# Seven block products for eight in every third pair of W_up's row tiles

## The chip, the cores and the metric

One core of a Trainium2 chip runs the whole program. The metric is the device time of one execution in microseconds (us), as the median of several runs.

## The reference

Two encoder layers on x of 512 positions by 1024 features. Each layer first mixes a Fourier group and windowed attention into x, and then runs the convolutional FFN, which is where the change lies (D_FF = 2816):

```python
h = rmsnorm(x, norm2[l])
up = dwconv_centred(h @ w_up[l], conv_w[l], conv_b[l])   # three taps along the positions
gate, val = up[..., :D_FF], up[..., D_FF:]
x = x + (jax.nn.silu(gate) * val) @ w_down[l]
```

W_up has 2 x 2816 columns, thus 44 row tiles of 128 in the transposed layout of the kernel. Tile fi of the gate and tile fi + 22 of the value belong together: a pair.

## The kernel before

Everything is kept transposed: features on the 128 partitions, the 512 positions along the free dimension. x is 8 tiles of 128 x 512. Inputs are float32, and the matmuls take operands of the reduced type fp32r. So each operand is split into a high part (a rounded copy, by ACT, line 101 or 137) and a low part (what is left, by DVE, line 102 or 140), and one product is three matmuls: high x high, low x high, high x low (`mm3`, lines 114 to 122). Weights are the stationary operand, and each matmul loads its own.

A tile of W_up (1024 x 128) is loaded as one transfer of 512 KB into `wraw` (3 buffers), split in two chunks of 512 columns into `whi` and `wlo` (5 buffers each, lines 132 to 141), and used for 8 contraction steps of 3 matmuls, 128 x 512 each, into one PSUM bank. The row scale 1/rms of h is applied afterwards (`rb2`, line 719), since it is a factor of each position. Then ACT does the middle tap and bias, DVE the two outer taps (lines 721 to 723). For a pair, ACT takes silu of the gate's tile, the two are multiplied (line 728: on DVE in layer 0, on POOL in layer 1), and the result is split into a high and a low part and kept as W_down's right operand.

The 22 pairs are done in two halves of 11 (`HALVES`, line 35). After each half comes W_down's part of it: for each of the 8 output tiles, 11 contraction steps of 3 matmuls into one bank, and an add into x (line 756). The kept operands lie in `slab`, `pT` and `m4` (lines 729 to 737). The last output tile of the last half is done in two halves of 256 positions (lines 748 to 756).

While layer 0's FFN runs, `presplit` (lines 149 to 198) prepares layer 1's weights other than W_up and W_down: it loads them, folds some of them on DVE, splits them (ACT and DVE, through `tA`) and stores both parts in DRAM. One step of it is taken at every `next(ahead)`: two in three pairs of tiles, and two for each output tile of W_down.

The order on each engine is fixed ahead of time by the framework's scheduler (line 841): it goes by the order of the program, and takes a later instruction where an earlier one is not ready by its own estimate. Each engine then runs its list in order. The accumulators of the FFN rotate over 6 PSUM banks (`FFN_BANKS`, line 34).

Of the kernel before, what the change touches and what calls it, by code (L numbers as in the profile page):

```python
# [31 lines left out]
NWARM = 10  # L32
RATE, STEP0 = 1, 12
FFN_BANKS = ("mm", "mm", "mm", "av", "sc", "sc")
HALVES = [(0, 11), (11, 11)]


def encoder_kernel(tc, t):
# [29 lines left out]
    def f(x):  # L68
# [2 lines left out]

    BANKS = {"mm": 3, "sc": 2, "tp": 2, "av": 1}
    TEMPS = {"act": (1024, 8), "m4": (1024, 5), "slab": (1024, 4), "pT": (2560, 2),
             "tA": (512, 6), "tF": (512, 6), "sq": (512, 2)}
# [14 lines left out]
    def act(out, in_, func=AF.Copy, **kw):  # L89
        return nc.scalar.activation(out, in_, func, **kw)  # L90
# [36 lines left out]
    def wload(src, n, raw=None):  # L127
        raw = wtile() if raw is None else raw
        nc.sync.dma_start(raw[:, :n], src)
        return raw[:, :n]  # L130

    def wsplit(raw, eng=None, hi_eng=None):
        hi = wp.tile([P, 512], F32R, tag="whi", name=nm("whi"), bufs=5)
        lo = wp.tile([P, 512], F32R, tag="wlo", name=nm("wlo"), bufs=5)
        n = raw.shape[-1]
        if hi_eng is None:
            act(hi[:, :n], raw)
        else:
            hi_eng.tensor_copy(hi[:, :n], raw)
        tt(lo[:, :n], raw, f(hi)[:, :n], ALU.subtract, eng)  # L140
        return hi, lo

    def wchunks(src, n, step=512, eng=None):
        raw = wload(src, n)
        return [wsplit(raw[:, c:min(c + step, n)], eng) for c in range(0, n, step)]
# [3 lines left out]
    def presplit(l):  # L149

        late = []

        def keep(key, src):
            n = src.shape[-1]
            two = [temp(n, "tA", F32R) for _ in range(2)]
            split(two[0], two[1], src)
            kept[key] = [dp.tile([P, n], F32, tag=f"{key}{s}", name=nm("kept")) for s in range(2)]
            store()
            late.append(lambda: [nc.sync.dma_start(o, f(z)) for o, z in zip(kept[key], two)])

        def store():
            while late:
                late.pop()()

        def cols(src, n, step):
            def load():
                raw = temp(1024, "m4")
                nc.sync.dma_start(raw[:, :n], src)
                return [raw[:, c:c + step] for c in range(0, n, step)]
            return load  # L170

        def prepare(kind, raw):
            if kind == "u":
                return fold_wu(raw)
            return fold_wf(raw) if kind == "f" else raw

        jobs = []
        for grp in (1, 0):
            for kk in range(KT // 2):
                jobs.append((cols(t["w_qkv"][l, grp, kk], 768, 384), [f"qkv{grp}{2 * kk + i}" for i in range(2)]))  # L180
        for kk in range(KT // 2):
            jobs.append((lambda kk=kk: load_wu(l, kk, temp(1024, "m4")), [f"u{2 * kk + i}" for i in range(2)]))
        for j in range(NF):
            jobs.append((lambda j=j: [load_wf(l, j, temp(1024, "m4"))], [f"f{j}"]))
        for half in range(2):
            for mp in range(KT // 2):
                jobs.append((cols(t["w_o"][l, half, :, mp * 1024:(mp + 1) * 1024], 1024, 512),
                             [f"o{half}{2 * mp + i}" for i in range(2)]))
        got = jobs[0][0]()
        for n, (_, keys) in enumerate(jobs):  # L190
            for i, key in enumerate(keys):
                keep(key, prepare(key[0], got[i]))
                if i == len(keys) - 1 and n + 1 < len(jobs):
                    got = jobs[n + 1][0]()
                yield
        store()
        while True:
            yield
# [66 lines left out]
    mask = cut(pb, 3 * P)  # L265


    zero = temp(512, "sq")
    nc.vector.memset(zero, 0.0)
    warm = temp(512, "sq", F32R)  # L270
    act(warm, zero)
    wps = psum("sc")
    for _ in range(NWARM):
# [44 lines left out]
        return tab, alt, wt  # L318


    def add_square(acc, src, first, tag="sq"):
# [46 lines left out]
    def load_wu(l, kk, raw=None):  # L368

        raw = wtile() if raw is None else raw  # L370
        nc.sync.dma_start(raw.rearrange("p (k c) -> p k c", k=2),
                          t["w_in"][l, 2 * kk * P:2 * (kk + 1) * P, 0:FW].rearrange("(k p) c -> p k c", p=P))
        return [raw[:, k * 512:(k + 1) * 512] for k in range(2)]

    acc = accum()
    xg = [norm_tile(k, g1[:, 0, :], acc) for k in range(KT)]

    for l in range(L):
# [323 lines left out]
        if l == 0:  # L702
            tabs, alts, wt = load_tables(1)
        ahead = presplit(l + 1) if l < L - 1 else iter(lambda: 0, 1)
        for f0, nf in HALVES:
            gu = []
            for fi in range(f0, f0 + nf):
                ys_ = []
                n = fi - f0
                for z in range(2):  # L710
                    m = fi + z * FT
                    w = wchunks(t["w_up"][l, m], 1024)
                    nps[0] += 1
                    o = psum(FFN_BANKS[nps[0] % len(FFN_BANKS)])
                    for k in range(KT):
                        mm3(o, [q[:, (k % 4) * P:(k % 4 + 1) * P] for q in w[k // 4]], [h2[k][:, s, :] for s in range(2)],
                            k == 0, k == KT - 1)
                    u = temp(512, "tF")
                    tt(u, o, rb2, ALU.mult)
                    y = temp(512, "tF")  # L720
                    act(y, u, AF.Identity, scale=cw[:, l, 1, m:m + 1], bias=cb[:, l, m:m + 1])
                    stt(y[:, 1:], u[:, :-1], cw[:, l, 0, m:m + 1], y[:, 1:], ALU.mult, ALU.add)
                    stt(y[:, :-1], u[:, 1:], cw[:, l, 2, m:m + 1], y[:, :-1], ALU.mult, ALU.add)
                    ys_.append(y)
                    if (2 * n + z) % 3 == 2:
                        next(ahead)
                act(ys_[0], ys_[0], AF.Silu)
                tt(ys_[0], ys_[0], ys_[1], ALU.mult, nc.gpsimd if l else nc.vector)
                if n < 4:
                    a = pair("slab")  # L730
                elif n < 8:
# [3 lines left out]
                else:  # L735
                    a = pair("m4")
                split(a[:, 0, :], a[:, 1, :], ys_[0])
                gu.append(a)
            nxt = []
            for m in range(KT):  # L740
                next(ahead)
                next(ahead)
                w = []
                for c in range(0, nf, 8):
                    n = min(8, nf - c)
                    w += wchunks(t["w_down"][l, m, :, (f0 + c) * P:(f0 + c + n) * P], n * P)
                end = l == L - 1 and f0 + nf == FT
                nh = 2 if end and m == KT - 1 else 1
                for h in range(nh):
                    q0, q1 = h * S // nh, (h + 1) * S // nh  # L750
                    nps[0] += 1
                    o = psum(FFN_BANKS[nps[0] % len(FFN_BANKS)])[:, q0:q1]
# [97 lines left out]
```

## Time and profile before

| | |
|---|---|
| median of 3 runs | 1057.46 us (1056.27 to 1057.54) |
| profiled execution | 1056.14 us, its span 1054.3 us |
| FFN of layer 0 | from about 190 to 535 us of the span |
| FFN of layer 1 | from about 705 us to the end |
| DMA share in the span | 40.5% of 16 engines (queue q1) |

The profile is one execution. PE is TensorE, DVE is VectorE, ACT is ScalarE, POOL is GpSimd, SP is the engine that issues the transfers. The page gives the busy time of each engine, the chain of work that ended last, and the costliest groups of instructions: line, engine, operation, output<-input, count, then busy us, mean ns of one, and idle time ahead of it with what ended it. A table by stretches has the length first, then busy us (x instructions) for PE, PEld (weight loads), DVE, ACT and POOL, then the granted clock, the DMA share and GB/s. A timeline row has start, duration, engine, line, operation; the idle time before it and its releaser stand in brackets. A row "x2" merges two instructions. Matmuls overlap: the distance between starts is their price, not the duration.

### The profile page before, as it was taken

Reading aid. Unit: us, or ns where it says so; the run is one execution under the profiler, and the core shown is the slowest. Engines: PE = TensorE matmul, PEld = TensorE weight load, DVE = VectorE, ACT = ScalarE, POOL = GpSimd, SP = SyncE. Lnnn points to the kernel's source line nnn. Section 1 sums busy time; section 2 is a strip of 40 time slices with the busy share of each in tenths; the row PEclk is TensorE's granted clock in tenths of the full one; section 3 lists DMA queues with packets and bytes.
Section 4 is the critical chain, followed back from the end, with each engine's and each line's share of the span. In section 5 each row is a group of like instructions: output and inputs, shape, how many; then the busy total and the mean of one; then the engine's idle time right before and its main releaser. Section 6 shows DMA issues by size and latency. Waiting matters only on the chain.

```text
span 1054.3 us, 14425 instructions
## 1 busy us (share of the span) xinstructions
PE 1038.2 (98%) x5107; PEld 873.2 (83%) x5107; DVE 726.8 (69%) x1384; ACT 507.9 (48%) x939; POOL 90.8 (9%) x164
## 2 busy tenths in 40 slices
PE   8998999999999999999999999999999999999998
PEld 8986778888888888888899887888888888888887
DVE  8878768697767777777519775478877336878632
ACT  5339755455444445455423785246554224454421
POOL 0004410000000000000000152001101000101100
PEclk9999999999999999999999999999999999999999
DMA  7232152332269833239856313333332333332241
GB/s 273 83 115 87 58 193 81 100 100 96 78 226 353 324 100 101 89 114 322 280 181 221 113 62 99 122 100 94 101 101 74 96 115 100 98 101 82 82 150 48
DMA packets 60475, 140.03 MB, mean 133 GB/s; under 512 B 6642, under 2 KB 22258, under 8 KB 60404
## 3 DMA queue, kind: packets, MB, share of 16 engines
q1 hardware_dynamic: 60404, 139.12, 40.5%
q8 instruction: 40, 0.66, 0.3%
q14 instruction: 31, 0.25, 0.1%
HBM read 116.02 MB, written 23.07 MB: 132 GB/s over the span
## 4 chain that ended last, share of the span: by engine, by line
PE 93%; DVE 2%; DMA 2%; ACT 1%; issue 1%; POOL 0%; SPq 0%; ACTq 0%; DVEq 0%; POOLq 0%
PE ps L122 28%; PE ps L120 28%; PE ps L121 28%; PE ps L118 3%; PE ps L548 2%; PE ps L541 2%; PE ps L529 1%; DMA wraw<-in_w_qkv_dram 1%; PE ps L234 1%; PE ps L227 1%; ACT tA L90 0%; DMA x<-in_xT_dram 0%; DVE tA L533 0%; ACT act L90 0%; PE ps L500 0%
## 5 line engine op out<-in xcount | busy, mean ns | idle before, releaser
L90 ACT ACTIVATE whi<-wraw 128x512 fp32r<-128x512 f32 (+1 forms) x296 | 182.0, 616 | 290.8 <-PE ps L122 278.4
L120 PE MATMUL ps<-act,whi 128*128 128x512 f32 x768 | 298.9, 390 | 0.0
L121 PE MATMUL ps<-act,wlo 128*128 128x512 f32 x768 | 298.3, 389 | 0.0
L122 PE MATMUL ps<-act,whi 128*128 128x512 f32 x768 | 298.2, 389 | 0.0
L93 DVE TENSOR_TENSOR wlo<-wraw,whi 128x512 fp32r<-128x512 f32 (+1 forms) x304 | 219.7, 726 | 103.4 <-ACT whi L90 102.0
L122 PEld LDWEIGHTS ps<-act,whi 128*128 128x128 f32 x768 | 144.2, 188 | 30.1
L120 PEld LDWEIGHTS ps<-act,whi 128*128 128x128 f32 x768 | 144.2, 188 | 29.7
L121 PEld LDWEIGHTS ps<-act,wlo 128*128 128x128 f32 x768 | 144.2, 188 | 29.7
L96 DVE SCALAR_TENSOR_TENSOR tF<-tF,pb,tF 128x511 f32<-128x511 f32 x176 | 133.5, 763 | 11.1 <-ACT tF L90 8.7
L93 DVE TENSOR_TENSOR tF<-ps,rb 128x512 f32<-128x512 f32 x104 | 71.2, 689 | 77.9 <-PE ps L122 64.7
L120 PE MATMUL ps<-slab,whi 128*128 128x512 f32 (+2 forms) x212 | 82.2, 388 | 0.0
L122 PE MATMUL ps<-slab,whi 128*128 128x512 f32 (+2 forms) x212 | 79.9, 380 | 0.4 <-DVE slab L93 0.3
L121 PE MATMUL ps<-slab,wlo 128*128 128x512 f32 (+2 forms) x212 | 80.0, 378 | 0.0
L90 ACT ACTIVATE tF<-tF,pb 128x512 f32<-128x512 f32 x88 | 71.7, 816 | 11.3 <-DVE tF L93 4.6
L93 DVE TENSOR_TENSOR x<-x,ps 128x512 f32<-128x512 f32 (+1 forms) x49 | 32.9, 674 | 36.5 <-PE ps L122 36.3
L93 POOL TENSOR_TENSOR tF<-tF,tF 128x512 f32<-128x512 f32 x22 | 30.2, 1371 | 256.1 <-DVE tF L96 224.1
L120 PE MATMUL ps<-pT,whi 128*128 128x512 f32 (+1 forms) x132 | 50.5, 383 | 0.0
L121 PE MATMUL ps<-pT,wlo 128*128 128x512 f32 (+1 forms) x132 | 50.5, 383 | 0.0
L122 PE MATMUL ps<-pT,whi 128*128 128x512 f32 (+1 forms) x132 | 50.5, 383 | 0.0
L538 POOL TENSOR_SCALAR tA<-tA,den 128x256 f32<-128x256 f32 (+1 forms) x64 | 37.4, 590 | 145.1 <-DVE den L537 144.6
L533 DVE CUSTOM_DVE_ANT_0 tA<-ps,pb,nsink 128x256 f32<-128x256 f32 (+1 forms) x64 | 37.8, 603 | 14.5 <-PE ps L529 9.7
L122 PEld LDWEIGHTS ps<-slab,whi 128*128 128x128 f32 x212 | 39.7, 188 | 8.3 <-DVE slab L93 0.9
(178 smaller groups left out, 1485.0 us busy)
## 6 DMA issues: line engine op xcount, KB each, us to landing
wraw<-in_w_up_dram SPq DMA_DIRECT2D x88, 512.0 KB, 3.5
wraw<-in_w_down_dram SPq DMA_DIRECT2D x32, 512.0 KB, 3.7
kept<-tA SPq DMA_DIRECT2D x56, 256.0 KB, 5.7
whi<-kept SPq DMA_DIRECT2D x28, 256.0 KB, 3.0
wlo<-kept SPq DMA_DIRECT2D x28, 256.0 KB, 3.0
kept<-tA SPq DMA_DIRECT2D x32, 192.0 KB, 4.4
wraw<-in_w_down_dram SPq DMA_DIRECT2D x32, 192.0 KB, 2.4
wraw<-in_w_o_dram SPq DMA_DIRECT2D x8, 512.0 KB, 3.7
```

Of the source, the lines that this page charges most:

```text
L90: return nc.scalar.activation(out, in_, func, **kw)
L93: return (eng or nc.vector).tensor_tensor(out, a, b, op=op)
L96: return nc.vector.scalar_tensor_tensor(out=out, in0=a, scalar=s, in1=b, op0=op0, op1=op1)
L118: nc.tensor.matmul(out, a[0], b[0], start=start, stop=stop, **kw)
L120: nc.tensor.matmul(out, a[0], b[0], start=start, stop=False, **kw)
L121: nc.tensor.matmul(out, a[1], b[0], start=False, stop=False, **kw)
L122: nc.tensor.matmul(out, a[0], b[1], start=False, stop=stop, **kw)
L227: nc.tensor.matmul(pt[:, 2 * b:2 * b + 2], acc[:, b * P:(b + 1) * P], ones2, start=True, stop=True)
L533: nc.vector.tensor_tensor_reduce(out=pr[:, :n], in0=sc[:, :n], in1=mask[:, m0:m0 + n], scale=qs_scale[p][:, i, e:e + 1], scalar=nsink[:, l ...
L538: nc.gpsimd.tensor_scalar(pr[:, :n], pr[:, :n], den[:, i:i + 1], 1.0, op0=ALU.mult, op1=ALU.mult)
L541: tr = nc.tensor.transpose(pp[:, j * P:(j + 1) * P], pr[:, j * P:(j + 1) * P], ident)
L548: pv = nc.tensor.matmul(py[64 * e:64 * e + 64, i0 * P:(i1 + 1) * P], vp[:, j, 64 * g:64 * g + 64], pT[:, half, e, b0:b0 + 2 * (i1 - i0) + ...
```

## The change

For every third pair (fi = 2, 5, 8, 11, 14, 17, 20, in both layers) the two tiles of W_up are taken together as a 2 x 2 block matrix: the blocks are 4 of the 8 contraction tiles by one of the two row tiles. h is taken as 2 x 2 blocks too: 4 contraction tiles by 256 positions. The product of the two is done with seven block products in place of eight (`up_seven`), each of 4 contraction steps of 3 matmuls, 128 x 256. This takes sums of weight blocks (`s1` to `s4`, on DVE), sums of h's blocks (`sums_of_h`, once per layer, split like any operand), and sums of products. X and Y are the two halves of one PSUM bank, Z half of another; X goes on accumulating over four products and is read in between. All other pairs are done as before (`up_eight`).

The 22 pairs are in three groups (8, 7, 7) in place of two halves, so that W_down is passed three times, with 8, 7 and 7 contraction steps; the kept operands lie in `slab` and `pT` alone. The sums of h lie in `m4`, `ropetab`, `v`, `accA`, `accF` and a new tile. The product of gate and value is on DVE in both layers. The low parts of all weights are on DVE, as before. `presplit` loads one key at a time into buffers of its own, is stepped once for each pair and once for each output tile, and its high parts are put behind the last convolution or weight split in ACT's order (`pace`).

```diff
-HALVES = [(0, 11), (11, 11)]
+GROUPS = [(0, 8), (8, 7), (15, 7)]
+SEVEN = [range(2, FT, 3), range(2, FT, 3)]
...
-            act(hi[:, :n], raw)
+            pace[0] = act(hi[:, :n], raw).ins
...
-            split(two[0], two[1], src)
+            with tc.issue_after(pace[0]):
+                act(two[0], src)
+            tt(two[1], src, f(two[0]), ALU.subtract)
...
+    LO, HI = slice(0, 256), slice(256, 512)
+
+    def rooms():
+        for _ in range(5):
+            z = temp(1024, "m4", F32R)
+            yield from (z[:, :512], z[:, 512:])
+        z = sp.tile([P, 1024], F32R, tag="ropetab", name=nm("room"), bufs=1)
+        yield from (z[:, :512], z[:, 512:])
+        for tag in ("v", "accA", "accF", "room"):
+            yield cp.tile([P, 512], F32R, tag=tag, name=nm("room"), bufs=1)
+
+    def sums_of_h(l, h2):
+        room = rooms()
+        out = []
+        for k in range(4):
+            b = [temp(512, "tF") for _ in range(2)]
+            for i in range(2):
+                act(b[i], x[k + 4 * i], scale=g2[:, l, k + 4 * i:k + 4 * i + 1])
+            t13, t24 = temp(512, "tF"), temp(512, "tF")
+            tt(t13[:, LO], b[0][:, HI], b[0][:, LO], ALU.subtract)
+            tt(t13[:, HI], b[1][:, HI], b[0][:, HI], ALU.subtract)
+            tt(t24[:, LO], t13[:, LO], b[1][:, HI], ALU.subtract)
+            tt(t24[:, HI], t24[:, LO], b[1][:, LO], ALU.add)
+            r13, r24 = [next(room), next(room)], [next(room), next(room)]
+            split(*r13, t13)
+            split(*r24, t24)
+            out.append(dict(B11=[z[:, LO] for z in halves(h2[k])], B21=[z[:, LO] for z in halves(h2[k + 4])],
+                            B22=[z[:, HI] for z in halves(h2[k + 4])], T1=[z[:, LO] for z in r13],
+                            T3=[z[:, HI] for z in r13], T2=[z[:, LO] for z in r24], T4=[z[:, HI] for z in r24]))
+        return out
+
+    def up_seven(l, fi, h2, ts, rb2):
+        a, b = [wload(t["w_up"][l, fi + z * FT], 1024) for z in range(2)]
+        a11, a12, a21, a22 = a[:, :512], a[:, 512:], b[:, :512], b[:, 512:]
+        xy, zz = bank(), bank()
+        X, Y, Z = xy[:, LO], xy[:, HI], zz[:, LO]
+        ua, ub = temp(512, "tF"), temp(512, "tF")
+
+        def product(o, w, key, start=False):
+            for k in range(4):
+                mm3(o, [z[:, k * P:(k + 1) * P] for z in w], ts[k][key], start and k == 0, k == 3, skip_group_check=True)
+
+        product(X, wsplit(a11), "B11", True)
+        act(ua[:, LO], X)
+        s1, s2, s3, s4 = [temp(512, "tA") for _ in range(4)]
+        tt(s1, a21, a22, ALU.add)
+        product(Y, wsplit(s1), "T1")
+        act(ub[:, HI], Y)
+        tt(s3, a11, a21, ALU.subtract)
+        tt(s2, s3, a22, ALU.subtract)
+        product(X, wsplit(s2), "T2")
+        act(ua[:, HI], X)
+        product(Z, wsplit(a12), "B21", True)
+        tt(ua[:, LO], ua[:, LO], Z, ALU.add)
+        product(X, wsplit(s3), "T3")
+        tt(ub[:, HI], ub[:, HI], X, ALU.add)
+        tt(s4, a12, s2, ALU.add)
+        product(Y, wsplit(s4), "B22")
+        tt(ua[:, HI], ua[:, HI], Y, ALU.add)
+        tt(ua, ua, rb2, ALU.mult)
+        yield ua
+        product(X, wsplit(a22), "T4")
+        tt(ub[:, LO], X, rb2[:, LO], ALU.mult)
+        tt(ub[:, HI], ub[:, HI], rb2[:, HI], ALU.mult)
+        yield ub
...
-        for f0, nf in HALVES:
+        ts = sums_of_h(l, h2)
+        for f0, nf in GROUPS:
             gu = []
             for fi in range(f0, f0 + nf):
-                ys_ = []
                 n = fi - f0
...
+                ys_ = [conv(l, fi + z * FT, u) for z, u in enumerate((up_seven if fi in SEVEN[l] else up_eight)(l, fi, h2, ts, rb2))]
+                next(ahead)
                 act(ys_[0], ys_[0], AF.Silu)
-                tt(ys_[0], ys_[0], ys_[1], ALU.mult, nc.gpsimd if l else nc.vector)
+                tt(ys_[0], ys_[0], ys_[1], ALU.mult)
...
             for m in range(KT):
                 next(ahead)
-                next(ahead)
-                w = []
-                for c in range(0, nf, 8):
-                    n = min(8, nf - c)
-                    w += wchunks(t["w_down"][l, m, :, (f0 + c) * P:(f0 + c + n) * P], n * P)
+                w = wchunks(t["w_down"][l, m, :, f0 * P:(f0 + nf) * P], nf * P)
```

`bank()` takes the next of the 6 rotating banks, `up_eight` and `conv` hold the loop body of before (`conv` records its ACT instruction in `pace`).

More of the change, by code (lines that the diff above doesn't have):

```diff
@@ L130, in wload @@
         return raw[:, :n]
+    pace = [None]
     def wsplit(raw, eng=None, hi_eng=None):
@@ L163, in store, with load @@
                 late.pop()()
[L165 to L175, printed above, removed]
+        def load(src):
+            raw = temp(512, "praw")[:, :src.shape[-1]]
+            nc.sync.dma_start(raw, src)
+            return raw
@@ L177, in presplit @@
         jobs = []
         for grp in (1, 0):
[L179 to L182, printed above, removed]
+            for k in range(KT):
+                c = (k % 2) * 384
+                jobs.append((f"qkv{grp}{k}", lambda g=grp, k=k, c=c: load(t["w_qkv"][l, g, k // 2, :, c:c + 384])))
@@ L189, in presplit @@
[L189 to L195, printed above, removed]
+            for m in range(KT):
+                jobs.append((f"o{half}{m}", lambda h=half, m=m: load(t["w_o"][l, h, :, m * 512:(m + 1) * 512])))
+        got = jobs[0][1]()
+        for n, (key, _) in enumerate(jobs):
+            raw = got
+            if n + 1 < len(jobs):
+                got = jobs[n + 1][1]()
+            keep(key, fold_wu(raw) if key[0] == "u" else fold_wf(raw) if key[0] == "f" else raw)
+            yield
@@ new lines, in up_eight @@
+    def up_eight(l, fi, h2, ts, rb2):
+        for z in range(2):
+            m = fi + z * FT
+            raw = wload(t["w_up"][l, m], 1024)
+            w = [wsplit(raw[:, c:c + 512]) for c in (0, 512)]
+            o = bank()
+            for k in range(KT):
+                mm3(o, [q[:, (k % 4) * P:(k % 4 + 1) * P] for q in w[k // 4]], [h2[k][:, s, :] for s in range(2)],
+                    k == 0, k == KT - 1)
+            u = temp(512, "tF")
+            tt(u, o, rb2, ALU.mult)
+            yield u
@@ L375, in encoder_kernel, with conv @@
+    def conv(l, m, u):
+        y = temp(512, "tF")
+        pace[0] = act(y, u, AF.Identity, scale=cw[:, l, 1, m:m + 1], bias=cb[:, l, m:m + 1]).ins
+        stt(y[:, 1:], u[:, :-1], cw[:, l, 0, m:m + 1], y[:, 1:], ALU.mult, ALU.add)
+        stt(y[:, :-1], u[:, 1:], cw[:, l, 2, m:m + 1], y[:, :-1], ALU.mult, ALU.add)
+        return y
     acc = accum()
```

42 lines of the change are left out of this document (12 added, 30 removed).

## The prediction, made before the changed kernel ran

> **What bounds the kernel now.** I read the page first (shares of the engines, the chain that ended last, the groups), then the table by stretches for the FFN of both layers, then the timeline of PE and DVE inside it.
>
> ```profile
> PE 1038.2 (98%) x5107; PEld 873.2 (83%) x5107; DVE 726.8 (69%) x1384; ACT 507.9 (48%) x939; POOL 90.8 (9%) x164
> PE 93%; DVE 2%; DMA 2%; ACT 1%; issue 1%; POOL 0%; SPq 0%; ACTq 0%; DVEq 0%; POOLq 0%
> 200.00:300.00 100.00, 100.00 (x443) 82.79 (x442) 81.59 (x124) 54.45 (x82) 0.00 (x0) 1.00 0.29 91
> 700.00:800.00 100.00, 100.00 (x451) 83.04 (x449) 77.88 (x106) 52.14 (x78) 13.60 (x10) 1.00 0.29 92
> L90 ACT ACTIVATE whi<-wraw 128x512 fp32r<-128x512 f32 (+1 forms) x296 | 182.0, 616 | 290.8 <-PE ps L122 278.4
> ```
>
> PE carries 93% of the chain. The stretch 200 to 300 us lies in layer 0's W_up: PE (first column after the length) never idles, DVE (third) is busy 82%, the granted clock is 1.00. The last row shows why nothing else matters there: ACT, which makes the high parts of weights, idles 279 us because a weight buffer is still held by a matmul. Weights are ready up to five buffers early; PE is the only bound, and DVE is the next.
>
> A matmul's duration overlaps the next one, so its price is the spacing. 443 matmuls of 512 columns start in 100 us: 0.2257 us each. For 256 columns the end of the kernel has a run of 66 that is the same kind of work (weights stationary, one load per matmul):
>
> ```profile
> 1042.98 0.28 PE L120 MATMUL ps<-slab,whi 128*128 128x256 f32 x1
> ...
> 1050.78 0.28 PE L122 MATMUL ps<-m,whi 128*128 128x256 f32 x1
> ```
>
> 65 spacings in 7.80 us: 0.120 us each, more than half of 0.2257. So seven eighths of the products are not seven eighths of the time.
>
> **Matmuls.** A pair by eight is 2 x 8 x 3 = 48 matmuls of 512: 48 x 0.2257 = 10.83 us. By seven it is 7 x 4 x 3 = 84 of 256: 84 x 0.120 = 10.08 us. Gain 0.75 us a pair; 7 pairs in each of 2 layers make 14: **-10.5 us**. (The Trainium skill, page "TensorE: Matmul & The Clock Gate", section "Back-to-back issue gap", gives N/2.4 + 2.5 ns, thus 109 and 216 ns, and the gain would be an estimated 16.6 us by it; the rows say 120 and 226, and the measurement decides.)
>
> **The five links inside a pair of seven.** X and Y are two halves of one bank, and the order is X, Y, X, Z, X, Y, X. Does the next product on the bank wait for the reader of the other half? In the Fourier stage, 8 matmuls write the two halves of one bank, 4 each, and ACT then reads the halves:
>
> ```profile
> 71.34 1.89 PE L118 MATMUL ps<-slab,tab 128*128 128x256 f32 x8
> 73.27 0.66 ACT L90 ACTIVATE slab<-ps 128x255 f32<-128x255 f32 x2 [1.34 <-PE ps L118]
> ```
>
> ACT sat idle for 1.34 us and began its first read only when all eight were done (71.34 + 1.89 = 73.23), though the first half was complete about a microsecond earlier. So engines are kept apart by bank, not by half. (The Trainium skill, page "PSUM — Partial Sum Buffer", section "PSUM bank collisions raise a hardware error", says that two engines on one bank and quadrant collide even on disjoint columns, so software has to keep them apart: it speaks against this change, and the trace agrees with the 1.34 us wait. Were halves enough, the next term would be near nothing.)
>
> One link, from the nearest rows:
>
> ```profile
> 1046.82 0.28 PE L122 MATMUL ps<-m,whi 128*128 128x256 f32 x1
> 1047.14 0.42 DVE L93 TENSOR_TENSOR x<-x,ps 128x256 f32<-128x256 f32 x1 [3.27 <-PE ps L122]
> L90 ACT ACTIVATE pT<-ps 128x256 f32<-128x256 f32 x32 | 12.1, 378 | 7.7 <-PE ps L541 7.3
> 73.94 2.77 PE L118 MATMUL ps<-slab,whi 128*128 128x258 f32 x12
> ```
>
> The reader starts 0.32 us after the last matmul's start, reads 0.38 (ACT) or 0.42 (DVE), and PE restarts at once (73.27 + 0.66 = 73.93, then 73.94). Less the normal spacing of 0.12: 0.6 us. Six products on the bank have five links: 3.0 us. Only Z, on its own bank, is free work of the pair: 12 x 0.12 = 1.44 us, which leaves 1.56 us. PE also takes matmuls of a later tile when one is not ready, as before's boundary between W_up and W_down shows (the m tile was late, and the next output's pT product is cut into):
>
> ```profile
> 820.85 0.39 PE L121 MATMUL ps<-pT,wlo 128*128 128x512 f32 x1
> 821.08 0.39 PE L120 MATMUL ps<-m,whi 128*128 128x512 f32 x1
> 821.30 0.39 PE L121 MATMUL ps<-m,wlo 128*128 128x512 f32 x1
> 821.53 0.39 PE L122 MATMUL ps<-pT,whi 128*128 128x512 f32 x1
> ```
>
> But it needs that tile's weights, and there are five buffers and seven products: the next pair's weights can only be there for the last two links. These two end in DVE adds, which can stand behind other DVE work of 0.6 us each. Bounds: nothing (all filled) to 1.56 + 2 x 0.6 = 2.8 us a pair, 0 to 39 us. I take 0.9 us a pair, between the full fill that before shows and the unfilled 1.56: **+12.6 us**.
>
> **DVE's load.** Its spacings, from dense stretches:
>
> ```profile
> 176.51 0.68 DVE L93 TENSOR_TENSOR tF<-ps,rb 128x512 f32<-128x512 f32 x1
> 177.11 0.68 DVE L93 TENSOR_TENSOR wlo<-wraw,whi 128x512 fp32r<-128x512 f32 x1
> 177.71 0.68 DVE L93 TENSOR_TENSOR x<-x,tF 128x512 f32<-128x512 f32 x1
> 236.94 1.53 DVE L96 SCALAR_TENSOR_TENSOR tF<-tF,pb,tF 128x511 f32<-128x511 f32 x2
> 238.51 0.69 DVE L93 TENSOR_TENSOR wlo<-wraw,whi 128x512 fp32r<-128x512 f32 x1
> 332.26 0.17 DVE L341 COPY tA<-m 128x2 f32<-128x2 f32 x1
> 332.34 0.75 DVE L93 TENSOR_TENSOR tA<-m 128x255 f32<-128x255 f32 x2
> 333.01 0.69 DVE L93 TENSOR_TENSOR wlo<-wraw,whi 128x512 fp32r<-128x512 f32 x1
> 807.07 0.55 DVE L93 TENSOR_TENSOR wlo<-wraw,whi 128x384 fp32r<-128x384 f32 x1
> 807.54 1.53 DVE L96 SCALAR_TENSOR_TENSOR tF<-tF,pb,tF 128x511 f32<-128x511 f32 x2
> ```
>
> 512 wide: 0.60; the two taps of a conv: 1.57; 256 wide: 0.335; 384 wide: 0.47; a fold of w_in: 0.75. A pair by eight: 4 low parts, 2 scalings, the product and its low part, 8 x 0.60, and two convs, 3.14: 7.9 us under 10.83 of PE. A pair by seven: 7 low parts, 4 sums of weights, 1 scaling, product and low part, 14 x 0.60; five half-wide adds and scalings, 1.68; two convs, 3.14: **13.2 us over 10.08 of PE**. Three pairs make 29.1 against 31.7: 92%, which fits only if work is moved into the neighbours. ACT needs 7 high parts, 3 half copies, 2 convs and 2 more, some 7 us, and stays free.
>
> Layer 0 adds the preparation of layer 1's weights: 8 keys of 384 wide (3.8 us) in the first group, 7 keys of u (0.60 + 0.75 each: 9.5) in the second, 7 of W_o (4.2) in the third; and the sums of h, 4 x (4 x 0.335 + 2 x 0.60) = 10.2, in the first. DVE against PE against PE before: group one 88.1 / 85.1 / 86.6; two 80.9 / 73.6 / 75.8; three 70.3 / 74.3 / 75.8. Layer 1 has only the sums: 84.3 / 85.1, 71.5 / 73.6, 66.1 / 74.3. So DVE is the bound in layer 0's first two groups. What it exceeds can run on into W_down, where it has two low parts, an add and a key, 2.4 us, in 5.4 of PE; at most it costs 1.5 + 5.1 = 6.6 us over before, at least nothing. The rows of the second group are far over, so: **+5 us**.
>
> **The sums of h at the start.** They stand ahead of the first weights in ACT's and DVE's order. DVE's idle time there in before:
>
> ```profile
> 189.94 1.90 DVE L93 TENSOR_TENSOR wlo<-wraw,whi 128x512 fp32r<-128x512 f32 x3 [3.35 <-ACT whi L90]
> 192.56 0.16 DVE L209 TENSOR_SCALAR nv<-ps 128x4 f32<-128x4 f32 x1 [0.72 <-PE ps L227]
> 194.03 0.69 DVE L93 TENSOR_TENSOR wlo<-wraw,whi 128x512 fp32r<-128x512 f32 x1 [1.31 <-ACT whi L90]
> 196.78 0.69 DVE L93 TENSOR_TENSOR wlo<-wraw,whi 128x512 fp32r<-128x512 f32 x1 [2.06 <-ACT whi L90]
> 199.91 0.69 DVE L93 TENSOR_TENSOR tF<-ps,rb 128x512 f32<-128x512 f32 x1 [2.43 <-ACT rb L90]
> ```
>
> 9.9 us idle against 10.2 of sums; queued behind them are the low parts that PE needs. Between 0 and 10.2 us a layer; by these rows near 1: **+2 us**.
>
> **Edits at nothing.** Three groups for two: one more boundary a layer, filled as at 820.85 above; unfilled, the chain from the last W_up matmul to the last low part less six covered k-steps is
>
> ```profile
> 810.88 0.39 PE L122 MATMUL ps<-act,whi 128*128 128x512 f32 x1
> 817.59 0.68 DVE L93 TENSOR_TENSOR wlo<-wraw,whi 128x512 fp32r<-128x512 f32 x1
> ```
>
> 6.7 - 6 x 3 x 0.2257 = 2.6 us, six times 16 at most. Eight more adds into x a layer (4.8 us of DVE) lie in W_down's slack. The product in layer 1 goes from POOL to DVE: 0.60 more on DVE a pair, but a low part beside POOL's product took 1.74 us in place of 0.69,
>
> ```profile
> 792.93 1.74 DVE L93 TENSOR_TENSOR wlo<-wraw,whi 128x512 fp32r<-128x512 f32 x1 [0.27 <-ACT whi L90]
> ```
>
> so DVE gains 0.45; PE never waited for either. Keys of layer 1 are loaded one by one (same bytes on SP's queue, share 0.29 in the stretch) and their high parts queued on ACT behind a conv: 44 keys in 46 calls, as before.
>
> **The sum.** -10.5 + 12.6 + 5 + 2 = +9 us. The profiled execution took 1056.14 us (span 1054.3 and 1.84 around it), 1.3 below the median of the runs; from the median 1057.46 + 9 = 1066.5, say **1067 us**.
>
> **Rivals.**
> First, *the links fill and DVE keeps up* (the other side, faster). Z and the next pair's matmuls fill the five links. For it: PE's order in before leaves no gap at all, and DVE's 92% leaves 2.6 us in three pairs. Against it: five buffers. It decides at an exposed time of 0.75 us a pair, the gain itself. With about 0.15 exposed and DVE's excess of layer 0 run into W_down: -10.5 + 2 + 2 = 1051 us. Chance 0.22.
> Second, *it evens out*: layer 1 gains its 5, layer 0's DVE excess takes 5 to 6.6 back: 1057 us. Chance 0.13.
> Third, *the chain stands in full*: the DVE adds that free the bank wait in DVE's own backlog, so links go unfilled, 1.56 + 0.3 a pair, 26 us, and layer 0's excess 6.6 and the start 5: 1057.5 - 10.5 + 38 = 1085 us. For it: DVE needs 13.2 us in a window of 10 to 12, and its order is fixed ahead of time. Chance 0.20.
> My forecast, 1060 to 1079, has 0.45.
>
> **Chances.** A difference under 0.2% (2.1 us) can hardly be told from none here. Faster by more: 0.22; within: 0.13; slower: 0.65. The range has to take in the first and most of the third: 1049 to 1091; the forecast's own is 1060 to 1079.
>
> **What would show it.** In the changed profile: pairs of seven with 84 matmuls at 0.120 (right) or wider; PE idle before L120, put down to ACT or DVE reading ua or ub, in clusters of five a pair (links), about 0.9 us a pair in total; idle put down to wlo (DVE's load), more in layer 0 than in layer 1, most in its second group; DVE busy above 95% in the groups' stretches; a gap near 190 us (sums). If PE stays without idle time in layer 1, the first rival holds. If the spacing at 256 columns is not 0.120, or PE reaches the other half of a bank while it is read, the sum is wrong at its root.

## The result, and the profile after

| | before | after |
|---|---|---|
| median | 1057.38 us | 1150.65 us (1147.69 to 1152.17) |
| profiled execution, its span | 1056.14, 1054.3 us | 1152.17, 1150.4 us |

The ratio is 1.088, 95% interval [1.0857, 1.0906]: slower by 93 us. The direction was forecast, the size was not: the time lies 60 us above the top of the range, further than the worst rival.

First the page of the changed kernel: busy time and instructions of each engine, the chain that ended last, and two groups (busy, mean ns | idle ahead, what ended it). L91 is the line of every ACT operation, L94 that of most DVE ones, L121 to L123 are the three matmuls of `mm3`; they were L90, L93 and L120 to L122.

```profile
PE 1064.2 (93%) x5599; PEld 910.9 (79%) x5599; DVE 813.5 (71%) x1624; ACT 549.2 (48%) x1055; POOL 65.3 (6%) x142
PE 66%; DVE 18%; issue 8%; ACT 4%; DMA 3%; POOLq 1%; POOL 0%; SPq 0%; DVEq 0%; ACTq 0%
L91 ACT ACTIVATE whi<-wraw 128x512 fp32r<-128x512 f32 (+1 forms) x282 | 169.5, 613 | 291.8 <-PE ps L123 256.5
L121 PE MATMUL ps<-m,whi 128*128 128x256 f32 x140 | 46.2, 330 | 47.2 <-ACT whi L91 25.3 <-ACT tF L91 21.8
```

PE's share of the chain fell from 93% to 66%, and DVE took 18%. Yet ACT still idles 292 us ahead of the high parts, held by matmuls: weights as such are not late. The fourth row is the key. Tile `m` holds most of the sums of h (T1 to T4), so these 140 matmuls stand inside pairs of seven, and 47 us of PE's idle time lie ahead of them. The same two stretches by the clock, in the table by stretches (the second holds less of the FFN than before, since layer 1's FFN starts some 60 us later):

```profile
200.00:300.00 100.00, 86.09 (x440) 74.61 (x438) 77.09 (x128) 51.28 (x88) 0.00 (x0) 0.91 0.43 133
700.00:800.00 100.00, 87.19 (x433) 72.08 (x431) 68.29 (x120) 46.26 (x82) 11.43 (x6) 0.95 0.30 93
```

PE was busy 100 of 100 us in both, now 86 and 87. The granted clock fell from 1.00 to 0.91 and 0.95. And DVE is *less* busy than before in the stretch that is W_up in both kernels, the first (77 against 82): it waits as well. That is not what an engine looks like that is the bound all the time.

Where the time went, from all rows of PE's timeline. A row joins matmuls of one group; what it takes beyond its matmuls' normal price (0.227 us each for 512 columns, 0.120 for 256, less for narrower ones) counts as a gap when it is over 0.3 us, as slow spacing from 0.05 to 0.3. Only the differences are used:

| | gaps | slow spacings |
|---|---|---|
| before | 39.1 us | 17.8 us |
| after | 122.6 us | 40.3 us |

83.5 more of gaps, 22.5 more of slow spacings, less the 10.5 that the matmuls give: 95.5 us, against 96.1 between the spans. So the sum closes, and the gap sum can be split. The groups of PE's lines for layer 0's stretch (190 to 560 us):

```profile
L121 PE MATMUL ps<-m,whi 128*128 128x256 f32 x70 | 23.0, 329 | 25.8 <-ACT whi L91 25.3 <-ACT tF L91 0.5
L122 PE MATMUL ps<-m,wlo 128*128 128x256 f32 x70 | 23.6, 337 | 11.1 <-DVE wlo L94 11.1
```

and for layer 1's (from 690 us):

```profile
L121 PE MATMUL ps<-m,whi 128*128 128x256 f32 x70 | 23.1, 330 | 21.4 <-ACT tF L91 21.4
```

Two different waits. In layer 1 it is ACT's copy of X out of PSUM (`ua`, in tag `tF`); in layer 0 it is the weights of the second product, made from the sum s1. Both end at Y's first matmul. The timeline of one such place in layer 1, in the pair fi = 11 (start, us, engine, operation, idle before it; here and below, rows that the reading does not need are left out):

```profile
940.07 0.28 PE L123 MATMUL ps<-act,whi 128*128 128x256 f32 x1
940.20 0.68 DVE L94 TENSOR_TENSOR tF<-ps,rb 128x512 f32<-128x512 f32 x1
940.80 0.73 DVE L97 SCALAR_TENSOR_TENSOR tF<-tF,pb,tF 128x511 f32<-128x511 f32 x1
941.46 0.68 DVE L94 TENSOR_TENSOR tF<-tF,tF 128x512 f32<-128x512 f32 x1
942.17 0.63 ACT L91 ACTIVATE slab<-tF 128x512 fp32r<-128x512 f32 x1 [0.40 <-DVE tF L94]
942.71 0.37 ACT L91 ACTIVATE tF<-ps 128x256 f32<-128x256 f32 x1
943.13 0.58 PE L121 MATMUL ps<-m,whi 128*128 128x256 f32 x1 [2.78 <-ACT tF L91]
943.51 0.41 PE L122 MATMUL ps<-m,wlo 128*128 128x256 f32 x1
943.72 0.41 PE L123 MATMUL ps<-m,whi 128*128 128x256 f32 x1
...
946.75 0.28 PE L122 MATMUL ps<-m,wlo 128*128 128x256 f32 x1
946.87 0.28 PE L123 MATMUL ps<-m,whi 128*128 128x256 f32 x1
```

Read it backwards. PE has done X's first product and Z by 940.07 and waits for the copy at 942.71. The copy waits for nothing of its own; it is behind a `slab` operation (942.17), the high part of the product of pair 9: the second `slab` row of this group, whose first pair is fi = 8. That waits for DVE's product of gate and value (941.46), which stands in DVE's list behind a scaling (940.20) and a tap (940.80) of pair 10. ACT runs its list in order, so the shortest job stands behind the tails of the two pairs before. After the wait the spacing is 0.21 us (943.51 to 943.72) and only from 946.75 on 0.12 again: half clock for 3 us.

The tails are late because DVE is in arrears at this point, though it is not over the whole stretch:

```profile
921.97 0.42 DVE L94 TENSOR_TENSOR tF<-tF,ps 128x256 f32<-128x256 f32 x1 [2.34 <-PE ps L123]
927.35 0.69 DVE L94 TENSOR_TENSOR tA<-wraw 128x512 f32<-128x512 f32 x1 [0.77 <-DMA wraw<-in_w_up_dram]
1050.43 0.69 DVE L94 TENSOR_TENSOR tF<-ps,rb 128x512 f32<-128x512 f32 x1 [1.36 <-PE ps L123]
```

From 921.97 to past the copy DVE stands idle only once for longer than 0.2 us, namely 0.77 us. Ahead of fi = 17, which does not wait at this link, it is DVE that waits for PE (1050.43). In layer 1 those pairs wait that have a pair of seven before them in their group (fi = 5, 11, 14, 20), and fi = 2 at the start; fi = 8 and 17, the first by seven of their groups, do not.

The same place in layer 0, in the pair fi = 5:

```profile
248.10 0.68 DVE L94 TENSOR_TENSOR tF<-ps,rb 128x512 f32<-128x512 f32 x1
248.87 0.81 ACT L91 ACTIVATE tF<-tF,pb 128x512 f32<-128x512 f32 x1 [2.53 <-DVE tF L94]
249.59 0.51 ACT L91 ACTIVATE tA<-praw 128x384 fp32r<-128x384 f32 x1
250.62 0.55 DVE L94 TENSOR_TENSOR tA<-praw,tA 128x384 fp32r<-128x384 f32 x1
251.09 0.68 DVE L94 TENSOR_TENSOR tA<-wraw 128x512 f32<-128x512 f32 x1
251.80 0.63 ACT L91 ACTIVATE whi<-tA 128x512 fp32r<-128x512 f32 x1 [0.39 <-DVE tA L94]
252.48 0.38 PE L121 MATMUL ps<-m,whi 128*128 128x256 f32 x1 [3.38 <-ACT whi L91]
254.16 0.68 DVE L94 TENSOR_TENSOR wlo<-tA,whi 128x512 fp32r<-128x512 f32 x1
254.89 0.58 PE L122 MATMUL ps<-m,wlo 128*128 128x256 f32 x1 [2.02 <-DVE wlo L94]
```

s1 (251.09, `tA<-wraw`) reads nothing but a loaded tile. On DVE it stands behind the low part of the presplit key (250.62), which needs the key's high part (249.59), which `pace` put behind the previous pair's conv on ACT (248.87), which waits for that pair's scaling (248.10). Then `wlo` stands behind four more operations of DVE. In all 5.4 us of idle for one pair.

For contrast, the pair fi = 8 of layer 1 is the first of its group; W_down lies ahead of it, and no pair's tail:

```profile
906.29 0.38 ACT L91 ACTIVATE tF<-ps 128x256 f32<-128x256 f32 x1 [0.80 <-PE ps L123]
...
907.41 0.28 PE L123 MATMUL ps<-act,whi 128*128 128x256 f32 x1
907.53 0.28 PE L121 MATMUL ps<-m,whi 128*128 128x256 f32 x1
...
908.85 0.28 PE L123 MATMUL ps<-room,whi 128*128 128x256 f32 x1
909.60 0.39 PE L121 MATMUL ps<-m,whi 128*128 128x256 f32 x1 [0.47 <-ACT tF L91]
```

ACT copies X while PE does Z, and Y starts at 907.53 without a gap. The second link takes 0.75 us from start to start, 0.63 above the normal spacing, as priced. The later ones are filled: this product of the same pair (913.88 to 915.19) stands between matmuls of 512 columns of the next tiles.

```profile
913.66 0.39 PE L123 MATMUL ps<-act,whi 128*128 128x512 f32 x1
913.88 0.28 PE L121 MATMUL ps<-m,whi 128*128 128x256 f32 x1
915.19 0.28 PE L123 MATMUL ps<-room,whi 128*128 128x256 f32 x1
915.31 0.40 PE L121 MATMUL ps<-act,whi 128*128 128x512 f32 x1
```

The first pair of seven in layer 1 (fi = 2) waits longest:

```profile
770.15 8.28 POOL L210 TENSOR_TENSOR nr<-nv,mhalf 128x4 f32<-128x4 f32 x1 [49.87 <-DVE nv L208]
...
793.13 0.58 PE L121 MATMUL ps<-m,whi 128*128 128x256 f32 x1 [7.18 <-ACT tF L91]
```

The row scale, a POOL operation on 128 x 4 that took about 1 us at most other places, took 8.28 us while DVE ran through the sums of h without a break. The first scalings come late, and the pair of seven waits 7.2 us at its first link. How much of that is due to the row scale, this trace does not show.

### The profile page after: what moved, and what is told of

Its sections match the earlier page's. It is cut to its first block, busy times and chain, and to the rows that moved or that the text cites. A ratio compares the mean times of both kernels' runs of the same rounds, so it can differ in the third digit from the quotient of the medians.

```text
span 1150.4 us, 15741 instructions
## 1 busy us (share of the span) xinstructions
PE 1064.2 (93%) x5599; PEld 910.9 (79%) x5599; DVE 813.5 (71%) x1624; ACT 549.2 (48%) x1055; POOL 65.3 (6%) x142
## 4 chain that ended last, share of the span: by engine, by line
PE 66%; DVE 18%; issue 8%; ACT 4%; DMA 3%; POOLq 1%; POOL 0%; SPq 0%; DVEq 0%; ACTq 0%
PE ps L121 20%; PE ps L122 20%; PE ps L123 19%; DVE tF L97 5%; DVE tF L94 3%; DVE tA L94 3%; PE ps L119 3%; DVE wlo L94 3%; DMA wraw<-in_w_up_dram 1%; PE ps L644 1%; ACT tA L91 1%; PE ps L625 1%; PE ps L637 1%; DVE tA L629 1%; DMA wraw<-in_w_qkv_dram 1%
## 5 line engine op out<-in xcount | busy, mean ns | idle before, releaser
L91 ACT ACTIVATE whi<-wraw 128x512 fp32r<-128x512 f32 (+1 forms) x282 | 169.5, 613 | 291.8 <-PE ps L123 256.5
L122 PE MATMUL ps<-act,wlo 128*128 128x512 f32 (+1 forms) x712 | 262.1, 369 | 0.4 <-DVE wlo L94 0.4
L94 DVE TENSOR_TENSOR wlo<-wraw,whi 128x512 fp32r<-128x512 f32 (+1 forms) x290 | 189.5, 664 | 102.5 <-ACT whi L91 100.4
L121 PE MATMUL ps<-act,whi 128*128 128x512 f32 (+1 forms) x712 | 260.9, 369 | 0.0
L123 PE MATMUL ps<-act,whi 128*128 128x512 f32 (+1 forms) x712 | 260.9, 368 | 0.0
L122 PEld LDWEIGHTS ps<-act,wlo 128*128 128x128 f32 x712 | 136.9, 192 | 22.5 <-DVE wlo L94 1.0
L121 PEld LDWEIGHTS ps<-act,whi 128*128 128x128 f32 x712 | 137.1, 192 | 21.4
L123 PEld LDWEIGHTS ps<-act,whi 128*128 128x128 f32 x712 | 136.8, 192 | 21.1
L121 PE MATMUL ps<-slab,whi 128*128 128x512 f32 (+2 forms) x276 | 105.7, 386 | 3.1 <-ACT slab L91 2.6
L122 PE MATMUL ps<-slab,wlo 128*128 128x512 f32 (+2 forms) x276 | 105.6, 383 | 1.8 <-DVE wlo L94 1.8
L123 PE MATMUL ps<-slab,whi 128*128 128x512 f32 (+2 forms) x276 | 105.3, 384 | 1.1 <-DVE slab L94 1.1
L91 ACT ACTIVATE tF<-tF,pb 128x512 f32<-128x512 f32 x88 | 71.3, 811 | 44.9 <-DVE tF L94 23.5
L121 PE MATMUL ps<-m,whi 128*128 128x256 f32 x140 | 46.2, 330 | 47.2 <-ACT whi L91 25.3
L94 DVE TENSOR_TENSOR tF<-ps,rb 128x512 f32<-128x512 f32 (+1 forms) x90 | 57.0, 642 | 36.3 <-PE ps L123 31.8
L94 DVE TENSOR_TENSOR x<-x,ps 128x512 f32<-128x512 f32 (+1 forms) x65 | 42.6, 675 | 56.4 <-PE ps L123 56.4
L121 PEld LDWEIGHTS ps<-m,whi 128*128 128x128 f32 x140 | 31.0, 222 | 52.5 <-ACT whi L91 26.6
L121 PEld LDWEIGHTS ps<-slab,whi 128*128 128x128 f32 x276 | 52.1, 189 | 14.6 <-ACT slab L91 3.5
L122 PE MATMUL ps<-pT,wlo 128*128 128x512 f32 (+1 forms) x163 | 62.9, 387 | 0.5 <-DVE wlo L94 0.5
L121 PE MATMUL ps<-pT,whi 128*128 128x512 f32 (+1 forms) x163 | 62.9, 387 | 0.1
L122 PEld LDWEIGHTS ps<-slab,wlo 128*128 128x128 f32 x276 | 52.2, 189 | 11.9 <-DVE wlo L94 2.1
L123 PEld LDWEIGHTS ps<-slab,whi 128*128 128x128 f32 x276 | 52.1, 189 | 11.8 <-DVE slab L94 1.9
```

Of the source, the lines that this page charges most:

```text
L94: return (eng or nc.vector).tensor_tensor(out, a, b, op=op)
L121: nc.tensor.matmul(out, a[0], b[0], start=start, stop=False, **kw)
L122: nc.tensor.matmul(out, a[1], b[0], start=False, stop=False, **kw)
L123: nc.tensor.matmul(out, a[0], b[1], start=False, stop=stop, **kw)
```

## The experiments

**Theory**: PE's idle time is the *first link* of each pair of seven (X's copy, and s1's two parts), whose ACT and DVE steps stand in order behind the tails of the pairs before; plus the start of each FFN. **Rivals**: DVE's load (13.2 us of work in 10.1), the regrouping, the `pace` rule.

Each ratio is to the kernel before, run beside it. "Base" of each diff is the changed kernel.

**All of the change but the sevens.**

```diff
-SEVEN = [range(2, FT, 3), range(2, FT, 3)]
+SEVEN = [(), ()]
```

> No pair by seven; the three groups, the sums of h (computed, not used) and the new preparation of layer 1's weights stay. Links or lump (both theories blame the pairs of seven): within 0.5% of before, 1055 to 1062 us, no PE idle of more than 1 us in the FFN, clock 1.00. Rival (regrouping, the later preparation or the sums of h cost much themselves): 1075 us or more, with PE idle at group boundaries.

1065.1 us, 1.008 [1.0058, 1.0104], 3 us above the range. 86 us of the loss need the sevens. But 8 remain, and not in the FFN: the stretch from 100 to 150 us, in the mixing of layer 0. Before:

```profile
100.00:150.00 50.00, 48.74 (x301) 37.57 (x301) 39.68 (x106) 37.22 (x98) 17.42 (x39) 1.00 0.39 123
```

With the regrouping alone:

```profile
100.00:150.00 50.00, 45.68 (x276) 35.26 (x275) 34.67 (x100) 33.51 (x91) 16.39 (x40) 0.97 0.10 32
```

Fewer matmuls in the same 50 us, at a stage that the change was not meant to touch. The diff had moved the temporaries of the squares (`add_square`) into the ring `tF`, to make room in SBUF; a ring that other work of that stage uses too. A later run gave them another one:

```diff
-    def add_square(acc, src, first, tag="tF"):
+    def add_square(acc, src, first, tag="praw"):
```

> As e1_eights (no pair by seven, 1065.1 us, 8.3 above before), but the squares for the norms take their temporaries from the two buffers of the new preparation, not from the ring tF that the change put them in. If the 8 us are that ring (its idle times lie in the mixing stages, not in the FFN): 1056 to 1060 us. If they are the sums of h or the third group: still 1063 us or more.

1055.43 us, 0.999 [0.9981, 0.9999], with PE busy again as before the change:

```profile
100.00:150.00 50.00, 48.75 (x304) 37.61 (x303) 36.50 (x103) 34.92 (x92) 18.62 (x41) 1.00 0.14 43
```

So the ring of the squares cost some 10 us (1065.1 to 1055.43), and the rest of the regrouping costs nothing that can be told: three groups, the product on DVE, the presplit loads, and the sums of h as well, which this kernel still makes and does not use.

**Sevens in layer 1 only** (`SEVEN = [(), range(2, FT, 3)]`).

> Pairs by seven in layer 1 alone, where nothing is prepared for a next layer. The FFN of layer 1 took 34.5 us more than before in the changed kernel, that of layer 0 61.3 us more. If the layers are independent: 1057 + 35 = 1085 to 1097 us, with one idle of about 2.8 us and one half clock stretch in each pair of seven after the first of a group. If the cost were only the prepared weights' excess on VectorE: within 1% of before.

1096.64 us, 1.038 [1.0362, 1.0398]. From 1065.1 that is 31.5 for layer 1's seven pairs, and to 1150.65 another 54.0 for layer 0's.

**A bank each for X, Y and Z.**

```diff
-        xy, zz = bank(), bank()
-        X, Y, Z = xy[:, LO], xy[:, HI], zz[:, LO]
+        X, Y, Z = bank()[:, LO], bank()[:, LO], bank()[:, LO]
...
-        product(Y, wsplit(s1), "T1")
+        product(Y, wsplit(s1), "T1", True)
```

> X, Y and Z each in a bank of its own, in both layers, so that a product waits only for the reader of its own output (three links of X, one of Y) and X to Y is no link. Links theory (the prediction's): most of the 96 us goes, 1060 to 1085 us. Lump theory (VectorE and ScalarE behind when a pair of seven starts): the 2.8 us idles after the first product in layer 1, which wait for ScalarE's copy of X, go or shrink, but those of layer 0, which wait for the split of the first sum of weights, stay: 1110 to 1135 us.

1111.74 us, 1.052 [1.0502, 1.0538]: 39 us back from three lines. Layer 1's 21.4 us fell to 1.3:

```profile
L121 PE MATMUL ps<-m,whi 128*128 128x256 f32 x70 | 20.0, 285 | 1.3 <-ACT tF L91 1.3
```

In layer 0 Y no longer waits for the copy either, but s1 is as late as before:

```profile
L121 PE MATMUL ps<-m,whi 128*128 128x256 f32 x70 | 23.7, 338 | 20.8 <-ACT whi L91 20.8
L122 PE MATMUL ps<-m,wlo 128*128 128x256 f32 x70 | 24.1, 345 | 8.7 <-DVE wlo L94 8.7
```

That separates the two waits: the shared bank is layer 1's, s1 is layer 0's.

**Less work on DVE**: the two outer taps of every conv are left out (`conv` returns after the middle tap), 176 of DVE's operations.

> The two outer taps of the convolution are left out in all 88 tiles: 3.14 us less of VectorE a pair, 138 us in all; the matmuls, the links and the weights stay. Load or lump theory (VectorE behind is what PE waits for): PE idles nearly vanish, 1046 to 1060 us. Links theory: links are as exposed as before, 1085 us or more.

1115.93 us, 1.055 [1.053, 1.0577]. DVE's busy time fell by 111 us (813.5 to 702.0), the time by 35. In layer 0 the same two waits stand, 18.9 and 8.2 us against 25.3 and 11.1:

```profile
L121 PE MATMUL ps<-m,whi 128*128 128x256 f32 x70 | 22.8, 326 | 19.4 <-ACT whi L91 18.9 <-ACT tF L91 0.5
L122 PE MATMUL ps<-m,wlo 128*128 128x256 f32 x70 | 23.1, 330 | 8.2 <-DVE wlo L94 8.2
```

So layer 0's wait is for the most part not DVE's load; that it is the order of its list, the next two runs show. In layer 1 the wait shrinks from 21.4 to 8.9 us. The first pair keeps 5.6 us; the waits of 2.6 to 2.8 us at the first link of the other four pairs are gone, and the rest is 0.47 us at each second link. There DVE's load counts: with less of it no arrears are left when the copy is due. A bank each removes the same four waits, so in layer 1 it takes both, the shared bank and the arrears.

**The keys out of W_up**: no presplit step in the pairs, two at each output tile of W_down.

```diff
-                next(ahead)
                 act(ys_[0], ys_[0], AF.Silu)
...
             for m in range(KT):
                 next(ahead)
+                next(ahead)
```

> The changed kernel, one bank for X and Y, with all steps of the preparation of layer 1's weights moved from the pairs of W_up to the output tiles of W_down, two at each. In layer 0 a pair of seven idled 2.8 + 1.4 us or more for the first sum of weights and its low part. Queue theory (the first sum shares a ring with the key just prepared and stands behind it on VectorE, which stands behind the last pair's convolution): those two idles go, the FFN of layer 0 falls from 410 us to about that of layer 1 (380), 1115 to 1130 us in all. If the sum was late for its transfer from memory or for VectorE's load: 1140 us or more, or the same idles.

1134.82 us, 1.074 [1.0726, 1.0755], between the two forecasts. Layer 0's waits for s1 and its low part (25.3 and 11.1 us) are gone, and the copy of X takes their place with 23.5:

```profile
L121 PE MATMUL ps<-m,whi 128*128 128x256 f32 x70 | 23.7, 339 | 23.5 <-ACT tF L91 23.5
```

Two waits lay over each other; taking away the later one shows the earlier.

**Without the rule `pace`** (the keys' high parts go where the scheduler puts them).

> The changed kernel, but the high parts of the prepared keys are no longer queued behind the last convolution on ScalarE. If that queueing alone puts the first sum late: as e6_keys_in_down, 1115 to 1130 us. If the shared ring does it (the key's store to memory frees the buffers only a pair later): little change, 1140 to 1155 us, with the same pairs of idles in layer 0.

1161.09 us, 1.099 [1.0974, 1.1004]: worse, and above both forecasts. In layer 0 PE now waits 46 us for the copy of X, and no longer for s1:

```profile
L121 PE MATMUL ps<-m,whi 128*128 128x256 f32 x70 | 24.4, 349 | 46.2 <-ACT tF L91 46.2
```

So `pace` decides which of the two steps is late, not whether one is: without keys in the pairs (the run before) the copy cost 23.5 us, with them 46.2 here. The ring `tA`, which s1 shares with the key, is still shared in this run, so the ring is not what held s1.

**Three banks, keys in W_down and squares in `praw` together**, with all fourteen pairs of seven.

> Three banks, keys in W_down and squares off tF together, pairs by seven in both layers. If these three are the whole of the loss and add up: 1111.7 - 7 x 5 (layer 0's two idles and their half clock) - 8 = 1063 to 1072 us, the rest being the idles at the first pair of seven of each layer. Were the load of VectorE itself the cause (13.2 us of it in a pair of seven): 1085 us or more.

1075.02 us, 1.017 [1.016, 1.0187]: 76 of the 93 us are back, and the time lies 3 us above the range forecast. 0.8 us is left ahead of the `m` matmuls in each layer. The gaps sum to 60.8 us against 39.2 for the eights with the same ring, the slow spacings to 25.1 against 18.2: 28.5 less 10.5 is 18.0, and the spans differ by 17.3. Of the 21.6 us of gaps, 16.3 lie at the start of the two FFNs, around the late row scale. Layer 0's row scale, and PE's wait for it (3.08 us in layer 1):

```profile
199.35 3.94 POOL L210 TENSOR_TENSOR nr<-nv,mhalf 128x4 f32<-128x4 f32 x1 [42.71 <-DVE nv L208]
203.34 1.74 PE L233 MATMUL ps<-ident,nr 128*128 128x128 f32 x8 [3.87 <-POOL nr L210]
```

**The start**, in three runs on that kernel: the first pair of seven at fi = 5 (`range(5, FT, 3)`, 12 pairs in all); the same with the sums of h made in quarters ahead of the pairs 1 to 4; and the sums alone moved, all behind the first pair, with the sevens from fi = 2.

> As the kernel with three banks, two keys at each tile of W_down and the squares in the praw ring (1075.0), but the first pair of seven in each layer is fi = 5, so 12 pairs of seven and not 14. The sums of h stay ahead of the first weights. Theory 1 (the start of each FFN carries the rest: the sums of h are an unbroken stretch of VectorE under which GpSimd's row scale and the first scalings come late, and the first pair of seven finds that backlog; 8.4 + 7.9 us idle there and the half clock behind it): the backlog is worked off by the eights of fi = 3 and 4, but the late row scale itself stays: 1050 to 1062, idle left only within 15 us of the row scale. Rival (VectorE's load over the whole FFN is the bound): two pairs fewer give back a seventh of the 29 us that the kernel lies over the eights' 1055.4 less 10.5: above 1069.

> As the one before (first pair of seven fi = 5), and the sums of h are made one quarter ahead of each of the pairs fi = 1, 2, 3 and 4 in place of all four ahead of the first weights. Theory 1 (the start is all that is left): no gap at the row scale, and the time falls to the eights' 1055.4 less 12 x 0.75 us: 1046.4, between 1044 and 1050, below the kernel before. Rival (VectorE's load): the same amount of work, so the same time as the one before, above 1060.

> As the kernel with three banks, two keys at each tile of W_down and the squares in the praw ring (1075.0), the first pair of seven again fi = 2, but the sums of h are made behind the first pair in program order. Theory 1, if the place of the sums is what makes the start late: GpSimd's row scale takes about 1 us again and the idle near 200 and 727 us falls, but the sums then stand within two pairs of their use: 1048 to 1062. If it is the first pair of seven's nearness to the start, whatever the place of the sums: 1068 to 1078.

Measured: 1060.66 us, 1.0024 [1.0012, 1.0036]; 1075.78 us, 1.0167 [1.0153, 1.0181]; 1087.82 us, 1.0282 [1.0268, 1.0296]. The first is as the theory had it (1050 to 1062): a backlog that two more pairs of eight work off. The other two are misses, each some 26 us above the top of theory 1's range, and each slower than the kernel from which it moves the sums (by 15 us, and by 12 to 13). POOL's row scale took 1.01 us in both, as expected, but the later sums of h are late themselves. The second of the three, layer 0:

```profile
240.63 0.58 PE L121 MATMUL ps<-room,whi 128*128 128x256 f32 x1 [5.63 <-ACT room L91]
```

`room` holds the last of the sums: spread over four pairs, they stand in the ordered lists among those pairs' work and finish after their first use. So making the row scale fast by moving the sums costs more than it gives. What part of the 14.4 us between 1075.02 and 1060.66 was the row scale stays open: with the first seven at fi = 5 it is faster as well (1.38 us in layer 0, 3.19 in layer 1), and PE no longer waits for it. Shown is that the start is paid for when a pair of seven follows close behind the sums.

**A version for the FFN of layer 1 alone**, from fi = 5, with three banks and squares in `praw`.

> Seven only in layer 1 and from fi = 5 on (6 pairs), three banks, the squares in the praw ring; layer 0 by eights, keys as in the changed kernel. By the sum that the runs have borne out so far: the eights with the squares in the praw ring 1055.4, less 6 x 0.75 us of matmuls, plus the 2.5 us of idle that layer 1 kept at its first pair of seven (755 us) in the kernel with all of this in both layers: 1053.4, between 1051.5 and 1055, a ratio of about 0.997. Rival (what the pairs of seven give, VectorE's longer list takes back in layer 1 too): 1055.4 or more.

1056.66 us, 0.9997 [0.9988, 1.0006]: no difference from before, and a miss of the 1053.4. The profiled execution adds up (gaps 41.2, slow 19.0: 3.3 more than before, less 4.5 for six pairs, and the span is 1053.2 against 1054.3), but a gain of 1 us is within what the runs of one kernel differ by (1055.08 to 1058.32). The time lies where the rival put it, at 1055.4 or more; the trace does not show whether for the rival's reason. No version with pairs of seven is faster than before by what can be told.

## Why the prediction was wrong

**The matmuls, -10.5 us: right.** In the changed kernel 24 matmuls of 256 columns lie from 937.32 to 940.07 us; 23 spacings, 0.120 us. With most of the waits removed the account still closes with it: the kernel with the first seven at fi = 5 gains 9.0 on twelve pairs, loses 8.9 on gaps and 2.5 on slow spacings against the eights, thus +2.4, and its span is longer by 2.4 (1057.5 against 1055.1). The gain is thus there in the sum, and no run's time fell by it.

**The five links, +12.6 us: the failed step.** The mechanism, a bank that two products share, was right. The size was not, and its shape wasn't either: no cluster of five of 0.6 us, but one wait of some 3 to 7 us at the first link in eleven of the fourteen pairs (six in layer 0, where s1 ends last, five in layer 1, where the copy does), and little at the other four: 0.5 us of idle at the second in layer 1, and then the next tiles' matmuls fill. The step priced a link from rows where the reader was idle when the product ended (0.6 us), and said of ACT that it "stays free". ACT is free on average, 48%; but its list is in order, and the copy stands behind the tails of the pairs before. The step looked for such a queue only at the last two links, on DVE. The ones that matter were at the first. And it counted the shared bank but not s1, the first weight that is made and not loaded; in layer 0 that alone cost 25.3 + 11.1 us.

**The half clock: not priced at all.** The slow spacings grew by 22.5 us. It is paid behind the waits, so the links cost about a quarter more than their idle time.

**DVE's load, +5 us: wrong in kind.** It was priced in layer 0's first two groups, as work beyond PE's time. The forecast's signs were idle time put to `wlo`, more in layer 0 (so it came: 11.1 against 0), and DVE above 95% (it was at 77 from 200 to 300 us). In the run without taps, 111 us less of DVE leave layer 0's waits at three quarters. In layer 1, where the step saw no cost, the load did count, by arrears that delay the copy while PE waits for it at the shared bank. In the versions without the two waits the same work was no bound: with the first seven at fi = 5, PE idles at most 0.9 us at a time in the pairs of seven.

**The sums at the start, +2 us: mis-sized.** In the kernel without the other waits, 14.4 us go with a first seven that comes later (1075.02 to 1060.66), though it has two pairs fewer to gain from. The sums by themselves cost nothing, as the eights that carry them show; the cost comes with a pair of seven close behind them, and about 7 us of it is PE's wait for the row scale (3.87 and 3.08).

**Edits at nothing: right for what was listed** (1055.4 us with all of them), but one edit was not listed: the ring of the squares, some 10 us, in another stage.

**The rivals.** The third, with its chain in full, was the nearest, and stopped at 1085 because it too multiplied a bare link. The first, in which the links fill, is nearly right for four links of five.

## What to carry to other kernels

When a change makes a wait *inside* a unit of work that had none, price it by what stands ahead of the releasing instruction in its engine's list at that moment, not by the duration of that instruction nor by the engine's share of busy time. Look first at the first internal hand-over, since the tails of the units before are still in the lists there; an engine that is free on average can be in arrears at that moment. And follow every buffer that a diff moves to another ring, also where the stage is not the one that is changed.

## What the runs showed of the hardware

- After an idle time of 2.78 us (ahead of 943.13) PE ran at half rate for some 3 us (0.21 us per 256 columns in place of 0.12). The length doesn't decide alone: in the run with sevens in layer 1 only, 2.76 us ahead of 888.35 were followed by the full rate. The Trainium skill, page "TensorE: Matmul & The Clock Gate", section "What's actually happening", has a free-running window of about 3.4 us; that the same length has either outcome agrees with a window that runs free, but here less than 3.4 us of idle was enough.
- POOL's operation on 128 x 4 took 8.28 us beside an unbroken run of DVE operations with two SBUF inputs (to 777.56), against 1.01 us where the sums of h stood elsewhere. The Trainium skill, page "SBUF — State Buffer", section "SBUF: two separate sides", says that such an operation and one of GpSimd that reads SBUF lock each other out for a whole instruction; the 8.28 us agree in kind, but they span some fifteen DVE operations, not one.
